# Output projection of a hybrid decoder layer: block products by a Strassen-Winograd scheme in place of eight block products, with prepared weight blocks kept in DRAM

## The chip, the core and the metric

The kernel runs on one core of a Trainium2 chip. The metric is the time of one execution in device microseconds; it was measured in three runs and the median counts. The engines are named as in the profile: PE is the matmul engine, PEld its weight loads, DVE the vector engine, ACT the scalar engine, POOL the GpSimd engine, and SP the queue that issues nearly all transfers between DRAM and SBUF, the on-chip memory. PSUM is the memory into which PE accumulates, in banks of 128 x 512 numbers.

## The reference

One layer is computed for x of 2048 tokens by 1024 columns, in float32. One projection feeds three token mixers, and their outputs go side by side through the output projection, which is added to the scaled input and normalised:

```python
    h = jnp.einsum('bsd,de->bse', x, w_in)
    a_u, a_v, a_g, b_val, b_glu, b_g, c_q, c_f, c_i, c_g = jnp.split(h, offsets, axis=-1)
    y_a = _sgu_mixer(a_u, a_v, sgu_ln_g, sgu_ln_b, sgu_w, sgu_b) * jax.nn.silu(a_g)
    y_b = _conv_module(b_val, b_glu, conv_w, conv_b, conv_ln_g, conv_ln_b) * jax.nn.silu(b_g)
    y_c = _hgrn2_mixer(c_q, c_f, c_i, lb, hgrn_norm_g) * jax.nn.silu(c_g)
    y = jnp.concatenate([y_a, y_b, y_c], axis=-1)
    y = jnp.einsum('bse,ed->bsd', y, w_out)
    return _layernorm(DEEPNORM_ALPHA * x + y, post_ln_g, post_ln_b)
```

Branch A (256 columns) is a gated unit that mixes 128 positions of a chunk by a triangular matrix. Branch B (256) is a causal convolution of width 31. Branch C (512, four heads) is a gated linear recurrence in chunks of 64 positions. W_out is 1024 x 1024.

## The kernel before

**Numbers in two parts.** A float32 operand of a product is split into a high part, rounded to the format that PE multiplies in one pass, and the low rest. `split` (L142 to L144) casts the high part on ACT and subtracts on DVE. `three` (L199 to L202) makes one product of three matmuls: high by high, high by low and low by high, each 128 x 128 by up to 512 columns. `load_split` (L146 to L154) brings every such operand through raw buffers of 128 x 512, six in turn (`RAWB`), by DMAs on SP (L152), and splits each piece. `load_small` gives a weight of 1024 columns four pairs of buffers in turn (tags whi and wlo). `load_x` brings a group of 512 tokens of x, transposed, into the pairs xhi and xlo, of which there are two.

**Stages.** The 2048 tokens are four groups of 512, and two groups make a half (`hf`). Each half goes through branch B, branch A, the values of branch C (`values`, L343 to L348: 16 products of 24 matmuls with 256 columns, copied out by ACT), and then C's eight units: four heads by two groups (`hgrn_unit`). A unit has projections f, q and g by `proj_f` (24 matmuls of 512 columns into one of three banks with the tag mm), elementwise work on DVE and ACT (among it L355, L362 and L377), score matmuls (L398) and small matmuls for states. Branch B's convolution runs on DVE as 31 multiply-adds of 128 x 512 for each of four accumulations per half (L284), put out one by one beside the later branches at the distance `DTAP` on the program's clock, and branch A's unit (`sgu_unit`) mixes at L629. `rstd_of` (L226 and L227) makes the reciprocal root of a variance on POOL. Every branch stores its output, transposed, to the DRAM tensor y_dr through SP (`y_store`, L231).

**Output projection.** In half 2 W_out is loaded and split: its left 512 columns (woh, wol) at the last head of C, its right 512 columns (xhiwo, xlowo) into the buffers of an x group after the last use. Then sixteen token tiles of 128 follow (from L738). For each, all 1024 columns of y come back as two DMAs of 256 KB, are split, and 2 x 24 matmuls go into two banks (po). L755 adds the scaled x, which L745 loaded, to a bank's result, L758 takes statistics, L760 joins them, POOL makes the reciprocal root, L762 and L765 normalise 1024 columns in two passes, and L766 stores them. The last tile's right half is done in two pieces of 256 columns, so that the end is short.

**What sets the order.** A clock counts the matmuls that the program has written (`tick`), and work is put off by `later` until the clock passes. A scheduler then orders the instructions of each engine by its own estimate, except those that are pinned to the written order. Each engine goes through its list in that order.

## Time and profile before

| what | value |
|---|---|
| median of three runs | 951.6 us (949.56 to 952.94) |
| the profiled execution: its span | 948.6 us |
| PE busy | 932.0 us, 98% of the span, 6165 matmuls |
| DVE busy | 668.3 us, 70% |
| ACT busy | 339.3 us, 36% |
| POOL busy | 83.0 us, 9% |
| memory read and written | 60.32 MB and 16.78 MB |

The profiled execution's own time is its span, 948.6 us; the runs of the table's first line were timed around the whole execution. A group row of the profile names the line, the engine, the operation, what it writes and reads, the shape and how often, and then the busy time, the mean of one in ns, the idle time of the engine just before and what ended it. A timeline row has the start and the duration in us first. A window row has the stretch, its length, the busy time of PE, PEld, DVE, ACT and POOL (with the count of instructions), PE's granted clock as a share of full speed, the DMA engines' busy share and GB/s. The stages of half 1 begin at about 0 (B), 75 (A), 148 (values) and 196 us (C), those of half 2 at 400, 453, 525 and 573 us, and the output projection at 753 us, at first between C's last units.

### The profile page before, as it was taken

The numbers are of one execution on the slowest core, as the hardware profiler recorded it, in microseconds if no ns is written. First come the engines' busy times: TensorE is split into PE (matmuls) and PEld (weight loads), VectorE is DVE, ScalarE is ACT, GpSimd is POOL, SyncE is SP. The second block draws the span as 40 slices with busy tenths as digits, with TensorE's granted clock in tenths as the row PEclk, the third lists the DMA queues.
The fourth block names the chain that finished last, engine by engine and source line by source line (L and its number), as shares of the span: only waits on it lengthen the run. The fifth ranks groups of instructions, "written<-read, shape, count | busy, mean of one in ns | idle before, by whom it ended". The sixth has DMA issues, their size and how long they took to land.

```text
span 948.6 us, 15705 instructions
## 1 busy us (share of the span) xinstructions
PE 932.0 (98%) x6165; PEld 772.7 (81%) x6165; DVE 668.3 (70%) x1561; ACT 339.3 (36%) x698; POOL 83.0 (9%) x130
## 2 busy tenths in 40 slices
PE   8999999999999999999999999999999999999996
PEld 5889889987777777788988998777777778888885
DVE  5998895146687669898899414668786965566554
ACT  6432333233354456552234223435455522110000
POOL 1001101000100000000210100010000012111211
PEclk9999999999999999999999999999999999999999
DMA  8401113111111104320111211201230734344221
GB/s 262 150 33 47 45 45 100 57 45 45 35 49 53 56 24 157 124 86 23 47 45 56 90 57 45 60 21 56 80 122 18 219 132 144 133 133 152 94 100 55
DMA packets 49993, 78.10 MB, mean 82 GB/s; under 512 B 4320, under 2 KB 20832, under 8 KB 49792
## 3 DMA queue, kind: packets, MB, share of 16 engines
q1 hardware_dynamic: 49872, 77.00, 24.8%
q8 instruction: 48, 0.79, 0.3%
q14 instruction: 25, 0.20, 0.1%
q0 software_dynamic: 48, 0.11, 0.1%
HBM read 60.32 MB, written 16.78 MB: 81 GB/s over the span
## 4 chain that ended last, share of the span: by engine, by line
PE 86%; DVE 8%; ACT 2%; issue 1%; DMA 1%; POOL 0%; SPq 0%; DVEq 0%; POOLq 0%; ACTq 0%
PE po L200 6%; PE po L201 6%; PE po L202 6%; PE pm_ci L200 3%; PE pm_ci L202 3%; PE pm_ci L201 3%; PE pm_q L200 3%; PE pm_q L201 3%; PE pm_q L202 3%; PE pm_f L200 2%; PE pm_f L202 2%; PE pm_f L201 2%; PE pm_cg L200 2%; PE pm_cg L201 2%; PE pm_cg L202 2%; PE pm_u L200 2%
## 5 line engine op out<-in xcount | busy, mean ns | idle before, releaser
L284 DVE SCALAR_TENSOR_TENSOR acc<-bh,vec,acc 128x512 f32<-128x512 f32 x240 | 172.8, 743 | 2.6
L144 DVE TENSOR_TENSOR wl<-rw,wh 128x512 fp32r<-128x512 f32 x84 | 56.7, 685 | 58.1 <-ACT wh L143 58.0
L143 ACT CAST wh<-rw 128x512 fp32r<-128x512 f32 x84 | 49.9, 618 | 42.5 <-PE pm_f L201 11.1
L755 DVE SCALAR_TENSOR_TENSOR rbuf<-rbuf,po 128x512 f32<-128x512 f32 (+1 forms) x33 | 22.1, 669 | 60.8 <-PE po L202 60.7
L200 PE MATMUL pm_ci<-wh_ci,xhix 128*128 128x256 f32 x192 | 54.8, 286 | 0.0
L202 PE MATMUL pm_ci<-wh_ci,xlox 128*128 128x256 f32 x192 | 54.3, 283 | 0.0
L201 PE MATMUL pm_ci<-wl_ci,xhix 128*128 128x256 f32 x192 | 54.3, 283 | 0.0
L200 PE MATMUL po<-xhiwo,wh_y 128*128 128x512 f32 (+1 forms) x136 | 52.2, 384 | 0.0
L143 ACT CAST wh_y<-rwy 128x512 fp32r<-128x512 f32 x32 | 18.6, 618 | 93.4 <-PE po L201 91.5
L201 PE MATMUL po<-xlowo,wh_y 128*128 128x512 f32 (+1 forms) x136 | 51.4, 378 | 0.0
L200 PE MATMUL po<-woh,wh_y 128*128 128x512 f32 x128 | 51.4, 401 | 0.0
L202 PE MATMUL po<-xhiwo,wl_y 128*128 128x512 f32 (+1 forms) x136 | 51.3, 377 | 0.0
L201 PE MATMUL po<-wol,wh_y 128*128 128x512 f32 x128 | 50.8, 397 | 0.0
L202 PE MATMUL po<-woh,wl_y 128*128 128x512 f32 x128 | 50.6, 395 | 0.0
L226 POOL TENSOR_SCALAR crs<-ss 128x4 f32<-128x4 f32 x16 | 3.6, 225 | 443.3 <-ACT jk L551 443.3
L200 PE MATMUL pm_f<-xhix,wh 128*128 128x512 f32 x96 | 41.0, 427 | 0.0
L200 PE MATMUL pm_q<-xhix,wh 128*128 128x512 f32 x96 | 40.9, 426 | 0.0
L201 PE MATMUL pm_q<-xlox,wh 128*128 128x512 f32 x96 | 39.3, 409 | 0.0
L200 PE MATMUL pm_cg<-xhix,wh 128*128 128x512 f32 x96 | 38.7, 403 | 0.0
L202 PE MATMUL pm_f<-xhix,wl 128*128 128x512 f32 x96 | 37.7, 393 | 0.0
L202 PE MATMUL pm_q<-xhix,wl 128*128 128x512 f32 x96 | 37.7, 393 | 0.0
L201 PE MATMUL pm_f<-xlox,wh 128*128 128x512 f32 x96 | 37.7, 393 | 0.0
(284 smaller groups left out, 2642.2 us busy)
## 6 DMA issues: line engine op xcount, KB each, us to landing
rw<-wf SPq DMA_DIRECT2D x84, 256.0 KB, 2.9
rwy<-y_dr SPq DMA_DIRECT2D x32, 256.0 KB, 3.7
rbuf<-x SPq DMA_DIRECT2D x16, 512.0 KB, 3.5
out<-rbuf SPq DMA_DIRECT2D x15, 512.0 KB, 2.6
rx<-xT SPq DMA_DIRECT2D x24, 256.0 KB, 3.5
rwci<-wt SPq DMA_DIRECT2D x16, 256.0 KB, 2.8
y_dr<-sg SPq DMA_DIRECT2D x16, 256.0 KB, 2.4
rwo<-wout SPq DMA_DIRECT2D x16, 256.0 KB, 2.9
```

Of the source, the lines that this page charges most:

```text
L143: nc.scalar.copy(hi, src)
L144: nc.vector.tensor_sub(lo, src, hi.bitcast(F32))
L200: nc.tensor.matmul(out, wh, xh, start=first, stop=False)
L201: nc.tensor.matmul(out, wh, xl, start=False, stop=False)
L202: nc.tensor.matmul(out, wl, xh, start=False, stop=last)
L226: nc.gpsimd.tensor_scalar(r, mv_var, scale, EPS, ALU.mult, ALU.add)
L284: nc.vector.scalar_tensor_tensor(a, h[:, k : k + G], vcol(cw + k), a, ALU.mult, ALU.add)
L755: nc.vector.scalar_tensor_tensor(r[:, ns], xn[:, ns], ALPHA, pt, ALU.mult, ALU.add)
```

## The change

**Seven products for eight.** A pair of token tiles is a 2 x 2 block matrix of y: a11 and a12 are the first tile's columns 0 to 511 and 512 to 1023, a21 and a22 the second's. W_out is a 2 x 2 block matrix too. The result is formed by the Winograd form of Strassen's scheme: four sums of y blocks (s1 to s4, on POOL), four of W_out's blocks, seven block products of 12 matmuls each (4 x `three`) and seven sums of products. Eight pairs take the place of sixteen tiles. The bank z accumulates four products, and ACT copies its state out in between (u1, u2, u4); the bank a holds one product and the bank dd two. DVE adds them into the tiles of x (xr).

**W_out's blocks.** `wo_prep` runs in half 1, in four steps behind the products 0, 4, 8 and 12 of `values`: it reads two rows of 512 KB of W_out, makes four sums on DVE, splits the seven blocks, and writes the high and low parts to the DRAM tensor wo_dr by 56 DMAs of 256 KB in all, 14.7 MB. `wo_load` brings a block back as two DMAs of 1 MB: blocks 0 to 2 into a new pool when C's pools are closed, 3 and 4 into the buffers of x's group 2, 5 and 6 into those of group 3, each when branch A has used that group for the last time.

**The order of half 2** becomes B, values, C, A; in half 1 it stays B, A, values, C. **Raw buffers** become three of 1024 columns, so most operands come and are split in pieces of 1024 instead of 512; the twelve first pieces of the program stay 512 wide. `DTAP` becomes 1.35 in half 2. The last tile's result is no longer cut into 256 columns.

```diff
-RAWB = 6
+RAWB = 3
...
-DTAP, DNORM = 1.5, 8.0
+DTAP, DNORM = (1.5, 1.35), 8.0
...
+    wo_dr = dr.tile([7, P, 2, 4 * 512], F32, name="wo_dr")
...
     def load_split(nm, hi, lo, srcs):
...
-            raw = wp.tile([P, 512], F32, tag="raw", bufs=RAWB, name=f"r{nm}_{k}")
+            raw = wp.tile([P, 1024], F32, tag="raw", bufs=RAWB, name=f"r{nm}_{k}")
+            n = src.shape[1] * (src.shape[2] if len(src.shape) == 3 else 1)
+            raw = raw[:, :n]
...
     def load_x(g):
-        return load_big(f"x{g}", [d["xT"][kt, :, g * G : (g + 1) * G] for kt in range(KT)])
+        return load_big(f"x{g}", [d["xT"][kt : kt + 2, :, g * G : (g + 1) * G]
+                                  .rearrange("k p t -> p k t") for kt in range(0, KT, 2)])
...
-    def values(hf, xs, vh):
+    def values(hf, xs, vh, between=lambda n: None):
...
+                    between(vp * 8 + gi * 4 + tt)
...
+    def wo_prep(pl, j):
+        raw = []
+        for e in range(2):
+            r = pl.tile([P, 1024], F32, tag="wr", bufs=2, name=f"wr{j}_{e}")
+            nc.sync.dma_start(r, d["wout"][:, j + 4 * e, :])
+            raw.append(r)
+        b11, b12 = raw[0][:, :512], raw[0][:, 512:]
+        b21, b22 = raw[1][:, :512], raw[1][:, 512:]
+        ta = pl.tile([P, 1024], F32, tag="wt", bufs=2, name=f"wta{j}")
+        tb = pl.tile([P, 1024], F32, tag="wt", bufs=2, name=f"wtb{j}")
+        t2, t3, t1, t4 = ta[:, :512], ta[:, 512:], tb[:, :512], tb[:, 512:]
+        nc.vector.tensor_sub(t1, b12, b11)
+        nc.vector.tensor_sub(t3, b22, b12)
+        nc.vector.tensor_sub(t2, b22, t1)
+        nc.vector.tensor_sub(t4, b21, t2)
+        for k, (src, blks) in enumerate(((b11, (0,)), (raw[1], (1, 5)), (ta, (2, 3)), (tb, (4, 6)))):
+            n = 512 * len(blks)
+            hi = pl.tile([P, 1024], F32R, tag="wh", bufs=2, name=f"wsh{j}_{k}")
+            lo = pl.tile([P, 1024], F32R, tag="wl", bufs=2, name=f"wsl{j}_{k}")
+            split(src, hi[:, :n], lo[:, :n])
+            for q, blk in enumerate(blks):
+                sl = slice(q * 512, (q + 1) * 512)
+                for hl, t in enumerate((hi, lo)):
+                    nc.sync.dma_start(wo_dr[blk, :, hl, j * 512 : (j + 1) * 512],
+                                      t[:, sl].bitcast(F32))
+    wo = [None] * 7
+    def wo_load(blk, t):
+        tv = t.bitcast(F32)
+        for k in range(2):
+            sl = slice(k * 1024, (k + 1) * 1024)
+            nc.sync.dma_start(tv[:, :, sl], wo_dr[blk, :, :, sl])
+        wo[blk] = t
...
+    def sgu(hf, xs, pl, after):
+        ws = [load_w(d["wt"][0, j], f"av{hf}_{j}") for j in range(2)]
+        vhat = sgu_values(hf, xs, pl, ws)
+        w = [load_wf(o, hf) for o in (A_U, A_G, A_U + 1, A_G + 1)]
+        for gi in range(GPH):
+            sgu_unit(hf * GPH + gi, gi, xs[gi], pl, vhat, w)
+            after(gi)
...
+            with ExitStack() as esa:
+                pl = pool(f"a{hf}", stack=esa, reuse_waits="tile")
+                sgu(hf, xs, pl, lambda gi: None)
+            with ExitStack() as esw:
+                pl = pool("wos", stack=esw, reuse_waits="tile")
+                values(hf, xs, vh, lambda n: wo_prep(pl, n // 4) if n % 4 == 0 else None)
...
+    def free_c(gi):
+        if gi == 0:
+            assert live[0] == 0
+            esc.close()
+            esv.close()
+            w1 = pool("w1", stack=es, reuse_waits="tile")
+            for blk in range(3):
+                wo_load(blk, w1.tile([P, 2, 4 * 512], F32R, name=f"wob{blk}"))
+            stiles.extend(w1.tile([P, 1024], F32, name=f"ysum{k}") for k in range(2))
+        for k, tag in enumerate(("xhi", "xlo")):
+            blk = 3 + 2 * gi + k
+            wo_load(blk, xp.tile([P, 2, 4 * 512], F32R, tag=tag, bufs=2, name=f"wob{blk}"))
+    stiles = []
+    with ExitStack() as esa:
+        pl = pool("a1", stack=esa, side="right", reuse_waits="tile")
+        sgu(NHALF - 1, xs, pl, free_c)
+    NP = S // (2 * P)
+    ot = pool("ot", stack=es, side="right", reuse_waits="tile")
+    gb = ot.tile([P, 2, DM], F32, name="gb")
     nc.sync.dma_start(gb, d["post"])
-    smp = pool("smp", stack=es)
-    for t in range(S // P):
-        yw = load_small(f"y{t}", [
-            y_dr[4 * j : 4 * j + 4, :, t * P : (t + 1) * P].rearrange("k p t -> p k t")
-            for j in range(2)])
...
-            pt = bank("mm", 3, f"po{t}_{n}_{c0}")[:, :w]
-            for kt in range(KT):
-                three(pt, yh[:, kt, :], yl[:, kt, :], wo[n][0][:, kt, c0 : c0 + w],
-                      wo[n][1][:, kt, c0 : c0 + w], kt == 0, kt == KT - 1)
-                tick(0.64 * w / 512)
...
+    def y_blocks(p):
+        raws = []
+        for k in range(2):
+            r = wp.tile([P, 1024], F32, tag="raw", bufs=RAWB, name=f"ry{p}_{k}")
+            t0 = (2 * p + k) * P
+            nc.sync.dma_start(r.rearrange("p (k t) -> p k t", t=P),
+                              y_dr[:, :, t0 : t0 + P].rearrange("k p t -> p k t"))
+            raws.append(r)
+        a11, a12 = raws[0][:, :512], raws[0][:, 512:]
+        a21, a22 = raws[1][:, :512], raws[1][:, 512:]
+        s2, s3 = stiles[0][:, :512], stiles[0][:, 512:]
+        s1, s4 = stiles[1][:, :512], stiles[1][:, 512:]
+        nc.gpsimd.tensor_tensor(s1, a21, a22, ALU.add)
+        nc.gpsimd.tensor_tensor(s2, s1, a11, ALU.subtract)
+        nc.gpsimd.tensor_tensor(s3, a11, a21, ALU.subtract)
+        nc.gpsimd.tensor_tensor(s4, a12, s2, ALU.subtract)
+        out = []
+        for k, src in enumerate((raws[0], stiles[0], stiles[1], a22)):
+            n = src.shape[1]
+            hi = wp.tile([P, 1024], F32R, tag="whi", bufs=4, name=f"wh_y{p}_{k}")
+            lo = wp.tile([P, 1024], F32R, tag="wlo", bufs=4, name=f"wl_y{p}_{k}")
+            split(src, hi[:, :n], lo[:, :n])
+            for q in range(n // 512):
+                sl = slice(q * 512, (q + 1) * 512)
+                out.append([t[:, sl].rearrange("p (k t) -> p k t", t=P) for t in (hi, lo)])
+        return dict(zip(("a11", "a12", "s2", "s3", "s1", "s4", "a22"), out))
+    def product(out, y, blk, first):
+        w = wo[blk].rearrange("p h (k n) -> p h k n", n=512)
+        for kt in range(4):
+            three(out, y[0][:, kt, :], y[1][:, kt, :], w[:, 0, kt, :], w[:, 1, kt, :],
+                  first and kt == 0, kt == 3, skip_group_check=not first)
+            tick(0.64)
+    def tmp(nm):
+        return ot.tile([P, 512], F32, tag="tmp", bufs=4, name=nm)
+    def normed(t, r, fine):
+        st = smp.tile([P, 2, 6], F32, tag="ost", bufs=2, name=f"ost{t}")
+        for n in range(2):
+            nc.vector.bn_stats(st[:, n, :], r[:, n * 512 : (n + 1) * 512])
         mv = smp.tile([P, 2], F32, tag="omv", bufs=2, name=f"omv{t}")
+        nc.vector.bn_aggr(mv, st)
         rs = rstd_of(smp, mv[:, 1:2], 1, "ors")
         nc.vector.scalar_tensor_tensor(r, r, mv[:, 0:1], gb[:, 0, :], ALU.subtract, ALU.mult)
+        for n in range(2 if fine else 1):
+            ns = slice(n * 512, (n + 1) * 512) if fine else slice(0, DM)
             nc.vector.scalar_tensor_tensor(r[:, ns], r[:, ns], rs, gb[:, 1, ns], ALU.mult, ALU.add)
             nc.sync.dma_start(d["out"][t * P : (t + 1) * P, ns], r[:, ns])
+    smp = pool("smp", stack=es, side="right")
+    n0, n1 = slice(0, 512), slice(512, 1024)
+    for p in range(NP):
+        y = y_blocks(p)
+        xr = []
+        for k in range(2):
+            t = 2 * p + k
+            r = ot.tile([P, DM], F32, tag="xr", bufs=4, name=f"xr{t}")
+            nc.sync.dma_start(r, d["x"][t * P : (t + 1) * P, :])
+            xr.append(r)
+        r1, r2 = xr
+        def plus(r, ns, t):
+            nc.vector.scalar_tensor_tensor(r[:, ns], r[:, ns], ALPHA, t, ALU.mult, ALU.add)
+        def join(r, ns, bk):
+            nc.vector.tensor_add(r[:, ns], r[:, ns], bk)
+        z = bank("mm", 3, f"poz{p}")
+        a = bank(("o", "st")[p % 2], 1, f"poa{p}")
+        dd = bank("sc", 2, f"pod{p}")
+        product(z, y["a11"], 0, True)
+        u1 = tmp(f"u1_{p}")
+        nc.scalar.copy(u1, z)
+        plus(r1, n0, u1)
+        product(a, y["a12"], 1, True)
+        join(r1, n0, a)
+        product(z, y["s2"], 2, False)
+        u2 = tmp(f"u2_{p}")
+        nc.scalar.copy(u2, z)
+        plus(r2, n0, u2)
+        product(dd, y["s3"], 3, True)
+        plus(r2, n1, dd)
+        product(z, y["s1"], 4, False)
+        u4 = tmp(f"u4_{p}")
+        nc.scalar.copy(u4, z)
+        nc.vector.tensor_add(r2[:, n1], r2[:, n1], u4)
+        product(dd, y["a22"], 6, False)
+        join(r2, n0, dd)
+        normed(2 * p + 1, r2, False)
+        product(z, y["s4"], 5, False)
+        plus(r1, n1, z)
+        normed(2 * p, r1, p == NP - 1)
```

Three places show how the engines' orders change. First ACT, at the end of half 1's values. `vh` takes the values (pm_ci), `wh` is a weight's high part, `f` and `X` are the first C unit's, and `wsh` are the high parts of W_out's blocks, from raw rows `wr` and sums `wta`, `wtb`. Before:

```order
L348 COPY vh<-pm_ci_1_1_2_1772 128x256
L143 CAST wh_0_1856<-rw_0_0_1858 128x512
L143 CAST wh_0_1856<-rw_0_1_1862 128x512
L348 COPY vh<-pm_ci_1_1_3_1800 128x256
L143 CAST wh_0_2188<-rw_0_0_2190 128x512
L143 CAST wh_0_2188<-rw_0_1_2194 128x512
L355 ACT_TABLE_LOAD
L355 ACTIVATE f_0_1895<-pm_f_0_1866 128x512
```

With the change:

```order
L354 COPY vh<-pm_ci_1_1_3_1892 128x256
L145 CAST wh_0_2269<-rw_0_0_2271 128x1024
L145 CAST wsh_3_1676<-wtb_1649 128x1024
L145 CAST wsh_0_1806<-wr_0_1796 128x512
L145 CAST wsh_1_1812<-wr_1_1798 128x1024
L145 CAST wsh_2_1820<-wta_1800 128x1024
L145 CAST wsh_3_1828<-wtb_1801 128x1024
L362 ACT_TABLE_LOAD
L362 ACTIVATE f_0_1976<-pm_f_0_1947 128x512
```

Five casts of W_out's blocks, those of the last step and one of the step before, now stand between the last value and `f` of the first C unit.

Second SP, where the output projection begins. Before, `rwo` are raw pieces of W_out, `rwy` of y, `gbb` the two vectors of the last normalisation, `rbuf` a tile of x, and y_dr takes the last outputs of C:

```order
L231 DMA y_dr<-sg_3_6585 128x512
L152 DMA rwo_6_7457<-wout 128x512
L152 DMA rwo_7_7461<-wout 128x512
L152 DMA rwy_0_7713<-y_dr 128x4x128
L152 DMA rwy_1_7717<-y_dr 128x4x128
L152 DMA rwy_0_7887<-y_dr 128x4x128
L152 DMA rwy_1_7891<-y_dr 128x4x128
L231 DMA y_dr<-sg_2_6877 128x512
```

With the change `wob` are W_out's blocks, in the order of their numbers 0 to 6, `ay` outputs of branch A, `xr` tiles of x and `ry` tiles of y:

```order
L237 DMA y_dr<-ay_2_7507 128x512
L713 DMA wob_7592<-wo_dr 128x2x1024 x2
L713 DMA wob_7595<-wo_dr 128x2x1024 x2
L237 DMA y_dr<-ay_2_7583 128x512
L713 DMA wob_7598<-wo_dr 128x2x1024 x2
L713 DMA wob_7603<-wo_dr 128x2x1024 x2
L713 DMA wob_7606<-wo_dr 128x2x1024 x2
L237 DMA y_dr<-ay_3_7675 128x512
L713 DMA wob_7747<-wo_dr 128x2x1024
L237 DMA y_dr<-ay_3_7744 128x512
L713 DMA wob_7747<-wo_dr 128x2x1024
L713 DMA wob_7750<-wo_dr 128x2x1024 x2
```

Behind these follow gb, both x tiles of pair 0 and the second y tile of pair 1 (ry_1_7914). The loads of W_out moved behind branch A's stores, and x, which stood behind the first tiles of y, stands behind all blocks.

Third DVE, in a steady stretch of the output projection. Before, one token tile:

```order
L755 SCALAR_TENSOR_TENSOR rbuf<-rbuf,po_0_0_8431 128x512
L758 BN_STATS ost_8430<-rbuf 128x6
L755 SCALAR_TENSOR_TENSOR rbuf<-rbuf,po_1_0_8458 128x512
L144 TENSOR_TENSOR wl_y_8716<-rwy_0_8717,wh_y_8715 128x512
L758 BN_STATS ost_8430<-rbuf 128x6
L144 TENSOR_TENSOR wl_y_8716<-rwy_1_8721,wh_y_8715 128x512
L760 BN_AGGR omv_8485<-ost_8430 128x2
L762 SCALAR_TENSOR_TENSOR rbuf<-rbuf,omv_8485,gbb 128x1024
L765 SCALAR_TENSOR_TENSOR rbuf<-rbuf,ors,gbb 128x1024
```

With the change, from the split of the next pair's s1 and s4 (`wl_y_2`) to the first sums of the next pair (`xr_8386`):

```order
L146 TENSOR_TENSOR wl_y_2_8379<-ysum_7602,wh_y_2_8378 128x1024
L838 SCALAR_TENSOR_TENSOR xr_8238<-xr_8238,omv_8330,gb 128x1024
L857 SCALAR_TENSOR_TENSOR xr_8236<-xr_8236,poz_8240 128x512
L841 SCALAR_TENSOR_TENSOR xr_8238<-xr_8238,ors,gb 128x1024
L834 BN_STATS ost_8351<-xr_8236 128x6
L146 TENSOR_TENSOR wl_y_3_8383<-ry_1_8364,wh_y_3_8382 128x512
L836 BN_AGGR omv_8354<-ost_8351 128x2
L857 SCALAR_TENSOR_TENSOR xr_8386<-xr_8386,u_4_8405 128x512
L838 SCALAR_TENSOR_TENSOR xr_8236<-xr_8236,omv_8354,gb 128x1024
L860 TENSOR_TENSOR xr_8386<-xr_8386,poa_8391 128x512
L841 SCALAR_TENSOR_TENSOR xr_8236<-xr_8236,ors,gb 128x1024
```

The normalising passes of two tiles now stand together, beside the splits and the first sums of the next pair.

More of the change, by code (lines that the diff above doesn't have):

```diff
@@ L152, in load_split @@
             nc.sync.dma_start(rv, src)
-            sl = slice(k * 512, (k + 1) * 512)
-            split(raw, hi[:, sl], lo[:, sl])
+            split(raw, hi[:, at : at + n], lo[:, at : at + n])
+            at += n
     def load_big(nm, srcs):
```

68 lines of the change are left out of this document (15 added, 53 removed).

## The prediction

> **What bounds the kernel now.** I read the page first, then the chain of waits, then stage windows and timelines. From the page:
>
> ```profile
> span 948.6 us, 15705 instructions
> PE 932.0 (98%) x6165; PEld 772.7 (81%) x6165; DVE 668.3 (70%) x1561; ACT 339.3 (36%) x698; POOL 83.0 (9%) x130
> PE   8999999999999999999999999999999999999996
> PEclk9999999999999999999999999999999999999999
> q1 hardware_dynamic: 49872, 77.00, 24.8%
> PE 86%; DVE 8%; ACT 2%; issue 1%; DMA 1%; POOL 0%; SPq 0%; DVEq 0%; POOLq 0%; ACTq 0%
> ```
>
> The reader is to see that TensorE (PE) is the bound in every slice but the first and the last, at full granted clock, and that 86% of the chain that ended last is PE. So whatever takes matmuls away shortens the run, as long as no other engine comes due in their place. DVE is next with 70%. The profiled execution spans 948.6 us; the median of the runs is 951.6, so about 3.0 us lie around the span. I work on the span and add 3.0. No change means within 0.3% of 951.6, that is 948.7 to 954.5.
>
> **1. The matmuls that go.** Starts of the first matmul of W_out half 0 (woh), of half 1 (xhiwo), and of the next token tile:
>
> ```profile
> 840.79 0.40 PE L200 MATMUL po<-woh,wh_y 128*128 128x512 f32 x1
> 846.39 0.39 PE L200 MATMUL po<-xhiwo,wh_y 128*128 128x512 f32 x1
> 851.86 0.40 PE L200 MATMUL po<-woh,wh_y 128*128 128x512 f32 x1
> ```
>
> A half is 24 matmuls: 5.60 us for woh (0.2333 each), 5.47 for xhiwo (0.2279). A tile is 11.07, so 16 tiles take 177.1 us for 768 matmuls. After, 8 pairs of 84 make 672. At the mean of 0.2306 that is 155.0, **-22.1 us**; at the two rates -20.3 to -24.0, since I cannot tell which rate the new places in SBUF get. A pair takes 19.1 to 19.6, I use 19.4.
>
> **2. The start.** The raw buffers become 3 of 1024 columns instead of 6 of 512, and the twelve first pieces stay 512 wide, so only three are in flight.
>
> ```profile
> 0.79 0.39 SPq L152 DMA_DIRECT2D rwfirst<-wf  x1
> 3.44 0.62 ACT L143 CAST whi_first<-rwfirst 128x512 fp32r<-128x512 f32 x1 [1.37 <-DMA rwfirst<-wf]
> 4.09 0.69 DVE L144 TENSOR_TENSOR wlo_first<-rwfirst,whi_first 128x512 fp32r<-128x512 f32 x1 [2.78 <-ACT whi_first L143]
> 20.49 0.39 PE L200 MATMUL pm_bg<-xhi_first,wh 128*128 128x512 f32 x1
> ```
>
> A buffer's round is issue to end of subtraction, 0.79 to 4.78: 4.0 us. Four rounds of three put the last split at about 17 to 19 us; PE's first two projections end at 20.5 today. So the twelve pieces are nearly hidden; the next weight comes as one 512 KB piece and is late by about **+1** (0 to +3).
>
> **3. W_out's sums during half 1's C values (wo_prep).** This adds work beside PE.
>
> ```profile
> 148.00:196.00 48.00, 48.00 (x399) 47.84 (x399) 11.82 (x22) 12.68 (x28) 2.54 (x6) 1.00 0.18 61
> 841.59 0.69 DVE L144 TENSOR_TENSOR wl_y<-rwy,wh_y 128x512 fp32r<-128x512 f32 x1
> 842.20 0.69 DVE L758 BATCH_NORM_STATS2 ost<-rbuf 128x6 f32<-128x512 f32 x1
> 840.76 1.14 ACT L143 CAST wh_y<-rwy 128x512 fp32r<-128x512 f32 x2 [9.93 <-PE po L201]
> 200.75 0.60 ACT L355 ACTIVATE f<-pm_f 128x512 f32<-128x512 f32 x1 [2.75 <-PE pm_f L202]
> 201.37 1.28 ACT L362 ACT_TABLE_LOAD   x1
> 206.19 0.69 ACT L362 ACTIVATE X<-pm_q 128x512 f32<-128x512 f32 x1 [3.54 <-PE pm_q L202]
> 211.52 0.76 PE L398 MATMUL sc<-X,K 128*32 128x80 f32 x32
> ```
>
> The first row is the values stage (columns PE, PEld, DVE, ACT, POOL, clock, DMA share, GB/s). A DVE subtraction of 512 occupies 0.61 from start to start, one of 1024 about 1.14 by doubling all but the fixed part. Each of four steps is 4 subtractions (2.4), one split of 512 (0.6) and three of 1024 (3.4): 6.4, in all 26 us of DVE; ACT casts 4 x (0.57 + 3 x 1.1) = 15.5 us. DVE is idle 36 of these 48 us and ACT 35, so the engines hide it. DMA does not: 4.2 MB of W_out are read, 14.7 MB written (7 x 128 x 2 x 2048 x 4 bytes), 2.1 MB are weights. The queue row gives 77.00 MB in 24.8% of 948.6 us, 327 GB/s while packets move: 21 MB are 64 us in a stage of 48. In ACT's order the last five casts stand ahead of f of the first C unit, and the last one waits until the writes two buffers back have landed: 19.4 MB, 59 us from 150, 2 to land, so 211, and 212 with its cast. Then follow 1.28 + 0.60 (table, f), 1.28 + 0.69 (table, X) and about 2 us of DVE (three operations of the size of L377 in point 6): scores at 218. PE starts its 16 score groups at 211.5 today; seven more matmuls stand ahead of them now, 1.6 us: 213. That is +5; at 367 GB/s (point 5) nothing. I take **+4** (0 to +9).
>
> **4. Branch A of half 2 behind C.** A and the values leave and enter with all their instructions; PE's work is the same. Less PE work now stands between branch B and C, in which the convolution must end.
>
> ```profile
> L284 DVE SCALAR_TENSOR_TENSOR acc<-bh,vec,acc 128x512 f32<-128x512 f32 x240 | 172.8, 743 | 2.6
> 431.63 0.69 DVE L259 TENSOR_TENSOR bh<-pm_val,bsig 128x512 f32<-128x512 f32 x1 [4.60 <-PE pm_val L202]
> 433.44 10.02 DVE L284 SCALAR_TENSOR_TENSOR acc<-bh,vec,acc 128x512 f32<-128x512 f32 x15
> L200 PE MATMUL pm_av<-wh_av,xhix x47: 278/283/283, 453.1 to 469.7; 128*128 128x256 f32 x47
> ```
>
> After 431.6 three of the four accumulations remain: 93 taps at 10.02 / 15 = 0.67 are 62 us, with eight splits (9) and a few multiplies 73: DVE is free at about 506. Then come branch B's statistics, about 5 us. PE leaves B at 453 (the first matmul of A today); with 48 for the values and two projections of 5.4 C's first X is due at 512. This is just covered: **0**, +4 if DVE is late, -1 since W_out's loads no longer disturb C's last head.
>
> **5. Reloading seven blocks and the first pair.** SP's order (with the change) has blocks 0 and 1 behind half 2's first y store of branch A, 2 to 4 behind its second, 5 and 6 behind its last; gb, x and pair 1's second y load stand behind all of them.
>
> ```profile
> 7.00:9.00 2.00, 1.14 (x4) 0.44 (x3) 1.00 (x2) 1.57 (x3) 0.00 (x0) 1.00 1.02 367
> 487.22 1.02 PE mix L629 x16
> ...
> 524.10 1.02 PE mix L629 x16
> rbuf<-x SPq DMA_DIRECT2D x16, 512.0 KB, 3.5
> ```
>
> The first and the last of four mixes stand 36.9 us apart, 12.3 each. Counting from A's first u projection, they lie at 12, 24, 36 and 48.5, PE is through at 49.3, and stores follow some 3 us behind. Blocks 0 to 4 (10.5 MB) are asked for from 18 on; at 340 GB/s, between 327 and 367, they run until 50. Blocks 5 and 6 can't start before x's buffers are free (48.3), nor the last before the store at 52. With gb, x and y 6.8 MB remain: 20 us, x of pair 0 at 68 to 70, pair 1's y at 71. PE has work until 71 from blocks that are there (the scheduler put pieces of pair 1 between). DVE needs x for its first sum, and four operations later (3 us) the bank of a22 is free: PE waits 0.6. The sums of pair 1 want three POOL additions, a cast and a split after 71: 77 against 74.4. With some catching up, **+4** (0 to +11).
> The Trainium skill (DMA: Bandwidth & Descriptors, Specifications) gives about 358 GB/s as the limit of a core's HBM traffic; the queue row's 327 lies under it, the two-microsecond row's 367 over it. By 358 this term would be about +3 as an estimate.
>
> **6. The steady pairs.** PE no longer waits for one sum at the end; seven products share two banks, and DVE has twice the split work per matmul (7 widths of 512 for 84, before 4 for 96). Rows that price DVE and POOL:
>
> ```profile
> 843.63 1.28 DVE L762 SCALAR_TENSOR_TENSOR rbuf<-rbuf,omv,gbb 128x1024 f32<-128x1024 f32 x1
> 843.68 1.28 POOL L226 TENSOR_SCALAR ors<-omv 128x1 f32<-128x1 f32 x1 [9.15 <-DVE omv L760]
> 845.63 1.29 DVE L765 SCALAR_TENSOR_TENSOR rbuf<-rbuf,ors,gbb 128x1024 f32<-128x1024 f32 x1 [0.72 <-POOL ors L227]
> 846.83 0.68 DVE L755 SCALAR_TENSOR_TENSOR rbuf<-rbuf,po 128x512 f32<-128x512 f32 x1
> 847.55 0.69 DVE L758 BATCH_NORM_STATS2 ost<-rbuf 128x6 f32<-128x512 f32 x1
> 249.98 0.58 DVE L377 TENSOR_TENSOR X<-X,f 128x256 f32<-128x256 f32 x1
> L226 POOL TENSOR_SCALAR crs<-ss 128x4 f32<-128x4 f32 x16 | 3.6, 225 | 443.3 <-ACT jk L551 443.3
> L584 POOL TENSOR_SCALAR_AFFINE_SELECT wm<-wm 128x512 f32<-128x512 f32 x1 | 1.0, 1025 | 20.1 <-DMA wm<-sguw 20.1
> ```
>
> From start to start: L765 1.20, L755 (PSUM) 0.72; statistics last as long as a split, 0.6; a tap is 0.67. ACT has 5.6 us a pair and is no bound. DVE's order has one tight loop: the split of the next pair's (s1,s4) waits until s4's product is over, since the buffer is the same, and from there the queue runs without a gap to the sum that frees a22's bank: cast 1.2, split 1.14, four normalising passes 4.8, sums and copies 0.72 + 0.65 + 0.7 + 0.65 + 0.72, statistics 0.8, splits 0.6 + 1.14: 13.1 us. PE gets to a22 five products after s4, at 13.8. So DVE fits with 0.7 us to spare, while POOL makes three of its four additions inside this stretch. No row shows such an addition; the nearest, L584, is 1.0 us. Whether it holds DVE up is open: L226 next to L762 takes 1.28, on a tile four times as wide but away from such DVE work 0.225, and ends as DVE ends, so the two exclude each other in one direction, while L377 started next to a POOL operation and ran at its usual 0.58. Bounds: nothing, or 3 x 1.0 - 0.7 = 2.3 us for each of 7 pairs, 16. In the stretch 2.7 us of DVE operations read only one SBUF operand and can lie beside POOL, so I take 1 us a pair: **+7** (0 to +16).
> The Trainium skill (SBUF — State Buffer, Who interferes with whom) says that a DVE instruction with two SBUF inputs and a GpSimd one that reads SBUF exclude each other, the first to start holding the port pair for its whole length. By that rule the L226 row agrees, additions hold DVE in turn, and the sum goes to the upper half of this range, as an estimate +12.
>
> **7. The end.** After the last matmul:
>
> ```profile
> 940.88 0.43 DVE rbuf L755
> ```
>
> The last sum is 512 wide, not 256 (0.72 for 0.43), so are its statistics (+0.2), and in DVE's order the other tile's last pass (1.2) stands between them: **+1.7** (1 to 2.5).
>
> Sum: -22.1 + 1 + 4 + 0 + 4 + 7 + 1.7 = -4.4. Three of these losses can't all be at their middle: the prep and pair 0 lose together by slow DMA, the loop by the port; where DMA is fast both of the first fall to 1 or 2. I put the likeliest at -6.6: 942.0 of span, **945 us**.
>
> **Rivals.** (a) *POOL's additions don't hold DVE.* Then term 6 is 0 and the time is 945 - 7 = 938; 935 if DMA also runs near 367. For: the L377 row. Against: the L226 row. (b) *The port becomes the bound, slower than before.* Every addition costs DVE its full length and DVE falls behind by 2.3 us or more a pair; with the fourth addition and L226's two beside the normalising passes, up to 3 us: 7 x 3 = 21 instead of 7, giving 959. It decides from 2.1 us of stall a pair on: 14.7 + the other 10.7 exceed 22.1 by 3.3, over 0.3%. (c) *DMA bound at both ends.* At 262 GB/s, the mean of the page's first slice (GB/s row below), the 17.3 MB from 18 on take 66 us, x lands at 86 instead of 70, +16 for +4, and the prep +9: 945 + 12 + 5 = 962.
>
> ```profile
> GB/s 262 150 33 47 45 45 100 57 45 45 35 49 53 56 24 157 124 86 23 47 45 56 90 57 45 60 21 56 80 122 18 219 132 144 133 133 152 94 100 55
> ```
>
> For: that slice was 84% busy. Against: it waits for buffers too, and packets of 2 KB and more moved faster elsewhere. (d) *The change doesn't shorten PE's queue*: excluded by the count, 672 for 768.
>
> **Chances.** Forecast 0.47 (940 to 950), (a) 0.24, (b) 0.16, (c) 0.13. The forecast's own range lies mostly under 948.7 (0.34 of 0.47), the rest within 0.3%; with (a) faster is 0.58; of (b) and (c) milder forms give 0.03 to no change, the rest is slower. So faster 0.58, same 0.16, slower 0.26. The range 935 to 958 holds (a), the forecast and the milder half of (b) and (c).
>
> **What would show it.** Right: 84 matmuls a pair at 0.228 to 0.233; the first scores of half 1 late by a few us behind ACT's casts; PE idle near the first pair for DMA or DVE; a22 waiting for DVE once a pair; POOL additions of 1 us or longer. Wrong: DVE idle in the steady pairs (then (a)); pairs of 21 us and more (then (b)); x of pair 0 landing over 30 us after branch A's last matmul (then (c)); PE waiting in branch B or C of half 2, which I hold covered.

## The result and the profile after

The changed kernel takes 966.8 us (964.45 to 970.7, four runs) against 951.56 us of the kernel before (949.56 to 952.94, four runs): a ratio of 1.0168, 95% interval 1.0141 to 1.0195. It is slower by 1.7%, where 945 us had been forecast. The profiled execution spans 964.8 us, 16.2 more than before. From its page:

```profile
span 964.8 us, 15346 instructions
PE 919.1 (95%) x6045; PEld 758.4 (79%) x6045; DVE 726.4 (75%) x1532; ACT 365.0 (38%) x658; POOL 134.4 (14%) x162
PE   7999999996999999999999999999999998899995
PEclk9999999997999999999999999999999999899998
q1 hardware_dynamic: 52368, 106.36, 32.6%
PE 59%; DVE 21%; DMA 9%; issue 4%; ACT 3%; POOL 3%; SPq 1%; DVEq 0%; POOLq 0%; ACTq 0%
```

PE's work did shrink, but PE's share of the chain that ended last fell from 86% to 59%: DVE and DMA stand in it now. The slices show where: the first, the tenth (217 to 241 us, where the granted clock falls too), the 34th and 35th (796 to 844 us) and the last. Windows make this sharper:

```profile
154.60:202.00 47.40, 47.40 (x398) 47.40 (x397) 26.22 (x36) 17.88 (x30) 0.89 (x2) 1.00 0.83 288
202.00:230.00 28.00, 20.75 (x109) 16.41 (x112) 17.88 (x28) 13.19 (x16) 1.19 (x3) 0.87 0.91 335
...
785.40:812.00 26.60, 24.75 (x105) 19.77 (x104) 9.06 (x13) 4.69 (x7) 3.00 (x3) 0.96 0.94 327
812.00:830.00 18.00, 12.04 (x47) 8.99 (x46) 14.32 (x17) 5.69 (x7) 12.80 (x10) 0.88 0.28 89
...
890.00:910.00 20.00, 20.00 (x90) 16.55 (x89) 19.24 (x24) 5.55 (x7) 10.84 (x8) 1.00 0.56 173
```

From 154 to 230 us the DMA engines are busy 83 to 91% of the time, and PE loses 7 us at the end of it. The output projection begins at 785.4: PE loses 2 and 6 us in its first 45 us. Between 850 and 890 us it loses 2.7 more. From 890 us on PE is busy all the time, although DVE is busy 19.24 us of 20. What PE waited for longest:

```profile
PE pod L206 <- DVE xr L857: 9.2, 4, 4.6
PE pm_f L206 <- ACT f L362: 5.8, 1, 5.8
```

To divide the 16.2 us, the same point of the program is sought in both traces: the first matmul of branch A, the first scores of C, the last matmul of half 2's branch B, the first and the last of the output projection. Before:

```profile
L200 PE MATMUL pm_av<-wh_av,xhi_first x32: 283/283/387, 75.6 to 86.8; 128*128 128x256 f32 x32
L398 PE MATMUL sc<-X,K x1024: 206/232/257, 211.5 to 761.2; 128*32 128x80 f32 x86, 128*32 128x48 f32 x85
L202 PE MATMUL pm_bg<-xhix,wl x32: 389/389/397, 393.0 to 452.9; 128*128 128x512 f32 x32
L200 PE MATMUL po<-xhiwo,wh_y x136: 280/389/504, 760.1 to 940.3; 128*128 128x512 f32 x120, 128*128 128x256 f32 x16
```

And after:

```profile
L206 PE MATMUL pm_av<-wh_av,xhi_first x32: 277/283/283, 82.7 to 93.8; 128*128 128x256 f32 x32
L405 PE MATMUL sc<-X,K x1024: 206/232/342, 229.2 to 709.8; 128*32 128x80 f32 x86, 128*32 128x48 f32 x85
L208 PE MATMUL pm_bg<-xhix,wl x32: 388/389/395, 413.1 to 473.1; 128*128 128x512 f32 x32
L206 PE MATMUL poz<-wob,wh_y x128: 388/389/499, 785.4 to 953.3; 128*128 128x512 f32 x128
```

The start is late by 7.1 us. By the first scores it is 17.7, so the preparation costs 10.6. By the end of half 2's branch B it is 20.2: another 2.5 in C of half 1. Before, the output projection's 177.1 us of matmuls would have filled the time from 763.7 to 940.8; now they begin at 785.4, late by 21.7: another 1.5 for the new order of half 2. The last matmul ends at 954.1: the projection takes 168.7 us. In it 12 matmuls in a row take 2.72 us (818.55 to 821.27 us), 0.2267 each, so 672 are 152.3: PE's saving is 24.8, and 16.4 are lost again. Behind the last matmul 10.7 us remain instead of 7.8: 2.9. The sum: 7.1 + 10.6 + 2.5 + 1.5 - 24.8 + 16.4 + 2.9 = 16.2.

How the preparation holds PE, in the timeline of ACT and then of PE:

```profile
216.18 0.62 ACT L145 CAST wsh<-wr 128x512 fp32r<-128x512 f32 x1 [8.61 <-DMA wr<-wout]
...
221.36 1.04 ACT L145 CAST wsh<-wtb 128x1024 fp32r<-128x1024 f32 x1 [0.90 <-DMA wo_dr<-wsh]
222.43 1.28 ACT L362 ACT_TABLE_LOAD   x1
223.72 0.60 ACT L362 ACTIVATE f<-pm_f 128x512 f32<-128x512 f32 x1
```

```profile
224.37 0.80 PE L206 MATMUL pm_f<-xhix,wh 128*128 128x512 f32 x1 [5.81 <-ACT f L362]
224.97 0.63 PE L207 MATMUL pm_f<-xlox,wh 128*128 128x512 f32 x1
225.39 0.63 PE L208 MATMUL pm_f<-xhix,wl 128*128 128x512 f32 x1
```

`f` of the first C unit stands behind the last casts of W_out's blocks on ACT, and these wait for DMA (8.61 us at one place). PE has all three mm banks full and waits 5.81 us for `f` to free one. Behind the wait the matmuls start 0.42 us apart instead of 0.227.

And the first pairs, from the timelines of DVE, POOL and PE:

```profile
806.30 0.69 DVE L857 SCALAR_TENSOR_TENSOR xr<-xr,u 128x512 f32<-128x512 f32 x1 [13.02 <-DMA xr<-x]
...
820.33 2.20 DVE L838 SCALAR_TENSOR_TENSOR xr<-xr,omv,gb 128x1024 f32<-128x1024 f32 x1
```

```profile
809.00 1.27 POOL L806 TENSOR_TENSOR ysum<-ry 128x512 f32<-128x512 f32 x1 [51.54 <-DMA ry<-y_dr]
...
821.40 2.27 POOL L807 TENSOR_TENSOR ysum<-ysum,ry 128x512 f32<-128x512 f32 x1
```

```profile
829.43 0.79 PE L206 MATMUL pod<-wob,wh_y 128*128 128x512 f32 x1 [4.60 <-DVE xr L857]
830.02 0.63 PE L207 MATMUL pod<-wob,wh_y 128*128 128x512 f32 x1
```

DVE stands idle for 13.02 us until x of pair 0 is there, the second y tile of pair 1 lands at 809.0, and from then on two pairs' sums, splits and normalising passes lie on DVE at once, beside POOL's additions. A 1024-wide pass takes 2.20 us where it met an addition, and an addition 2.27 where it met a pass, against 1.28 and 1.27. PE waits 4.60 us for a bank that DVE has not read, and again runs slowly behind it. Part of this wait is not DVE's work but POOL's order:

```profile
825.44 0.19 POOL L232 TENSOR_SCALAR ors<-omv 128x1 f32<-128x1 f32 x1
826.29 1.28 DVE L841 SCALAR_TENSOR_TENSOR xr<-xr,ors,gb 128x1024 f32<-128x1024 f32 x1 [2.08 <-POOL ors L233]
```

The variance for this pass, of a tile of pair 0, is there at 819.9, but POOL begins its reciprocal root only at 825.44, behind the additions of pair 2. DVE stands idle for 2.08 us, and the sum that frees PE's bank stands behind this pass in DVE's order. The chain of waits that leads to the matmul at 829.43 runs through the late loads of y, POOL's additions, this root and DVE's passes.

### The profile page after: what moved, and what is told of

Same layout as the page of the kernel before. It is cut to its first block, busy times and chain, and to the rows that moved or that the text cites. A ratio compares the mean times of both kernels' runs of the same rounds, so it can differ in the third digit from the quotient of the medians.

```text
span 964.8 us, 15346 instructions
## 1 busy us (share of the span) xinstructions
PE 919.1 (95%) x6045; PEld 758.4 (79%) x6045; DVE 726.4 (75%) x1532; ACT 365.0 (38%) x658; POOL 134.4 (14%) x162
## 4 chain that ended last, share of the span: by engine, by line
PE 59%; DVE 21%; DMA 9%; issue 4%; ACT 3%; POOL 3%; SPq 1%; DVEq 0%; POOLq 0%; ACTq 0%
DVE acc L290 4%; PE pm_q L206 3%; PE pm_q L207 2%; PE pm_q L208 2%; PE pm_f L206 2%; DMA wr<-wout 2%; PE pm_f L207 2%; PE pm_f L208 2%; DMA ry<-y_dr 2%; PE pm_cg L206 2%; DVE wl L146 2%; PE poz L208 2%; PE poz L207 2%; PE poz L206 2%; PE pm_ci L208 2%
## 5 line engine op out<-in xcount | busy, mean ns | idle before, releaser
L146 DVE TENSOR_TENSOR wl<-rw,wh 128x1024 fp32r<-128x1024 f32 x42 | 51.3, 1223 | 20.1 <-ACT wh L145 20.0
L145 ACT CAST wh<-rw 128x1024 fp32r<-128x1024 f32 x42 | 44.1, 1049 | 33.6 <-PE pm_f L207 12.6
L206 PE MATMUL poz<-wob,wh_y 128*128 128x512 f32 x128 | 50.0, 392 | 0.7 <-ACT wh_y L145 0.7
L208 PE MATMUL poz<-wob,wl_y 128*128 128x512 f32 x128 | 49.6, 390 | 0.6 <-DVE wl_y L146 0.6
L207 PE MATMUL poz<-wob,wh_y 128*128 128x512 f32 x128 | 49.8, 389 | 0.0
L558 ACT ACTIVATE jk<-po 128x128 f32<-128x128 f32 x64 | 17.7, 276 | 57.4 <-PE po L553 56.5
L207 PE MATMUL pm_f<-xlox,wh 128*128 128x512 f32 x96 | 38.7, 404 | 0.0
L208 PE MATMUL pm_f<-xhix,wl 128*128 128x512 f32 x96 | 38.7, 403 | 0.0
L208 PE MATMUL pm_cg<-xhix,wl 128*128 128x512 f32 x96 | 37.5, 390 | 0.0
L207 PE MATMUL pm_cg<-xlox,wh 128*128 128x512 f32 x96 | 37.5, 390 | 0.0
L207 PEld LDWEIGHTS pm_ci<-wl_ci,xhix 128*128 128x128 f32 x192 | 36.9, 192 | 0.0
L206 PEld LDWEIGHTS pm_ci<-wh_ci,xhix 128*128 128x128 f32 x192 | 36.9, 192 | 0.0
```

The costliest lines, as they stand in the source:

```text
L145: nc.scalar.copy(hi, src)
L146: nc.vector.tensor_sub(lo, src, hi.bitcast(F32))
L206: nc.tensor.matmul(out, wh, xh, start=first, stop=False, **kw)
L207: nc.tensor.matmul(out, wh, xl, start=False, stop=False, **kw)
L208: nc.tensor.matmul(out, wl, xh, start=False, stop=last, **kw)
L558: nc.scalar.activation(jk, po[:, c * P : (c + 1) * P], AF.Square, accum_out=ss[:, c : c + 1])
```

## The experiments

Theory A: the matmuls go as counted; the time is lost at the start by the raw buffers, in half 1 by the preparation's bytes, and in the first pairs by late x and y with POOL's additions on top. Its rivals were that DVE or POOL bounds the steady pairs, or that latency and order, not bytes, set the two DMA stages. All ratios are against the kernel before; with the changed kernel's 1.0168, one hundredth of ratio is 9.5 us.

**Raw buffers undone.** Pieces of 512 columns, two to a raw buffer, so six in flight:

```diff
-        for k, src in enumerate(srcs):
-            raw = wp.tile([P, 1024], F32, tag="raw", bufs=RAWB, name=f"r{nm}_{k}")
...
+                if not half:
+                    t = wp.tile([P, 1024], F32, tag="raw", bufs=RAWB, name=f"r{nm}_{k}")
+                    half.extend((t[:, :512], t[:, 512:]))
+                raw = half.pop(0)
```

> The changed kernel, with operands cut into pieces of 512 columns again; two pieces share one of the three raw buffers of 1024, so six are in flight. Theory A (the start is late because only three pieces are in flight, and the next x group waits for its own larger pieces): the first matmul of branch A comes at about 76 us instead of 82.7, and the time falls by 6 to 8 us, to about 960. Rival B (the first pieces are late for the speed of the DMA engines alone, or the delay is taken up later by a wait that is there anyway): first matmul of branch A later than 80, or the time falls by less than 3 us.

Measured: 1.0114 (1.0085 to 1.0142), about 5 us less than the changed kernel. The first matmul of branch A is at 76.1, as before the change:

```profile
L219 PE MATMUL pm_av<-wh_av,xhi_first x32: 283/283/388, 76.1 to 87.3; 128*128 128x256 f32 x32
```

The start is the raw buffers'. Of the 6.6 us won there 4.5 are left at the first scores (224.7): the preparation's first read came only 3.8 us earlier (156.5), and its last cast's end 4.7 (217.7).

**The raw buffers alone, in the kernel before.** `RAWB = 3`, tiles and pieces of 1024:

> The kernel before with the raw buffers alone changed: three of 1024 columns, pieces of 1024 except the twelve first. Theory A (this edit by itself makes the start late): first matmul of branch A at 80 to 85 us instead of 75.6, time higher by 4 to 8 us, about 957. Rival B (the late start needs the other edits): time within 2 us of the kernel before.

Measured: 1.0125 (1.01 to 1.0149), some 12 us, more than expected. The first matmul of A is at 80.2 (4.6 late), B of half 2 ends 7.2 late, the output projection ends 10.7 late. So the start is only part of it: here the larger pieces cost 2.6 us more between branch A of half 1 and branch B of half 2, and 3.5 behind that. The preparation took back some of what undoing them won in the changed kernel; why the rest was not won there stays open. Over all runs with three buffers the first matmul of A lies between 79.8 and 84.9 us, with six always between 75.6 and 76.2.

**Half the preparation's bytes.** Only the high parts are written, and the reload reads them twice:

```diff
-                for hl, t in enumerate((hi, lo)):
-                    nc.sync.dma_start(wo_dr[blk, :, hl, j * 512 : (j + 1) * 512],
-                                      t[:, sl].bitcast(F32))
+                nc.sync.dma_start(wo_dr[blk, :, 0, j * 512 : (j + 1) * 512],
+                                  hi[:, sl].bitcast(F32))
```

> The changed kernel, but only the high parts of the block sums are written to DRAM (7.3 MB for 14.7) and the reload reads them for both parts; all casts and subtractions of the preparation stay. The low parts of the weights are so left out of the result. Theory A (the preparation in half 1 is bound by its DMA bytes, and the last five casts on ACT hold the first forget gate f of branch C): the first scores come at about 221 instead of 229.2 and the time falls by 7 to 10 us, to about 958. Rival B (the chain of reads, casts and two buffers is bound by latency, whatever the bytes): scores later than 226 and the time falls by less than 4 us.

Measured: 1.0068 (1.0048 to 1.0088), 9.5 us less. In this run the first matmul of A is at 84.9, 9.3 later than in the kernel before, and the scores are late by 9.5:

```profile
L405 PE MATMUL sc<-X,K x1024: 206/232/257, 221.0 to 701.5; 128*32 128x80 f32 x86, 128*32 128x48 f32 x85
```

So with half the writes the preparation costs nothing, although all its casts still run ahead of `f`: they are over at 208.8 us instead of 222.4. It was bound by DMA, not by the chain of casts and buffers. Bytes and the count of writes fell together here; what speaks for the bytes is that, from the first read to the last cast, the DMA engines moved 286 GB/s over 46.2 us here and 317 GB/s over 62.1 us in the changed kernel: at a similar rate the length fell with the bytes.

**The y sums.** First without them:

```diff
-        nc.gpsimd.tensor_tensor(s1, a21, a22, ALU.add)
...
-        for k, src in enumerate((raws[0], stiles[0], stiles[1], a22)):
+        for k, src in enumerate((raws[0], raws[1], raws[0], a22)):
```

> The changed kernel without the four block sums on POOL; the splits read the blocks of y instead, so the result lacks the sums, while DVE, ACT and PE have the same instructions. Theory A (additions of 1.3 to 2.3 us stand between the second pair's y and its products and hold DVE's two-operand instructions): PE's losses from 812 to 890 us, about 9 us with the lower clock behind them, mostly go, and the time falls by 5 to 9 us, to about 960. Rival B (the first two pairs wait for DMA only, and PE is the bound from 890 us on, so the additions are covered): the time falls by less than 3 us.

Measured: 1.0037 (1.0024 to 1.005), 12.5 us less, more than theory A gave it. x comes no earlier (DVE waits 13.1 us for it), but the projection takes 156.6 us instead of 168.7, because DVE and PE catch up at once:

```profile
830.00:850.00 20.00, 20.00 (x90) 16.57 (x89) 18.79 (x26) 5.55 (x7) 5.65 (x6) 1.00 0.53 177
```

Then with the additions made, but read by nothing:

> As the run without the additions (the splits read the blocks of y, so the sums are missing from the result), but POOL makes its four additions per pair all the same, into tiles that nothing reads. Theory A (what costs is mainly the additions' place in the chain from y's load to the products: their latency): the time stays near the run without additions, 954 to 957. Rival B (what costs is mainly that they hold DVE's instructions): DVE's steady pairs are as long as in the changed kernel, and most of the 12.5 us return: 960 to 966.

Measured: 1.0253 (1.0225 to 1.0281), slower than the changed kernel by 8 us. It is not their place in the chain of y alone that costs:

```profile
PE pod L206 <- DVE xr L857: 19.7, 6, 8.9
L841 DVE SCALAR_TENSOR_TENSOR xr<-xr,ors,gb 128x1024 f32<-128x1024 f32 x15 | 24.3, 1617 | 8.1 <-POOL ors L233 7.9
```

The pass takes 1617 ns on average, and DVE waits 7.9 us for the reciprocal roots (2.8 in the changed kernel), which queue behind the free-running additions on POOL. Last, the additions on DVE (`nc.vector` for `nc.gpsimd`):

> The changed kernel with the four block sums of y on DVE instead of POOL, everything else the same. Theory A (POOL's additions cost by their length, 1.3 us alone and up to 2.3 beside DVE, and by holding DVE, more than DVE's own 4 x 0.6 = 2.4 us per pair): DVE then works about 18.2 us per pair of 19.1, PE stays the bound in the steady pairs, and the time falls by 7 to 12 us against the changed kernel, to about 957. Rival B (DVE has no room for 2.4 us more and becomes the bound): pairs of 20 us and more, time not lower than 964.

Measured: 1.0135 (1.0116 to 1.0155), about 3 us less: neither theory's number. Even these do not come from the sums: the projection of the profiled run takes 169.3 us, no less than in the changed kernel, and the first matmul of A is at 79.8 instead of 82.7. DVE still waits 12.91 us for x, and then has the sums to make besides two pairs' work. Where the sums are made matters little while x is late.

**SP's order.** Blocks 5 and 6 and gb behind x of pair 0:

```diff
-        sgu(NHALF - 1, xs, pl, free_c)
+        sgu(NHALF - 1, xs, pl, lambda gi: None if gi else free_c(gi))
...
-    nc.sync.dma_start(gb, d["post"])
...
+        if p == 0:
+            free_c(1)
+            nc.sync.dma_start(gb, d["post"])
```

> The changed kernel with blocks 5 and 6 and the post-normalisation vectors asked for behind the x tiles of pair 0 in the program, which puts x ahead of block 6 and of the vectors on SP's queue. Theory A (PE waits in the first pairs for the sum that needs x, because x stands behind the blocks): x lands at about 797 instead of 806, PE waits for the third accumulation of the first pairs by 4 us less, and the time falls by 3 to 5 us, to about 963. Rival B (the bytes bound it: what x gains, block 6 and the second pair's y lose): the time stays within 2 us.

Measured: 1.012 (1.0105 to 1.0135), 4.6 us less in the runs, but the projection of the profiled run is shorter by only 3.3. The wait moved:

```profile
PE poz L206 <- ACT wh_y L145: 8.6, 1, 8.6
```

Now the second pair's sums are late instead of the first pair's x: POOL makes them from 808.6 to 817.0, the first two in 2.0 and 2.2 us beside DVE's passes.

**Half the reload's bytes**, the preparation untouched; DVE zeroes the low halves:

> The changed kernel, but the reload brings only the high halves of the seven blocks (7.3 MB for 14.7) and DVE sets the low halves to zero, 2048 columns per block; the low parts of the weights are so left out of the result. The preparation in half 1 is untouched. Theory A (the output projection's 168 us come from the reload's bytes, which make x and y of the first pairs late, and from the catching up behind it): x lands before PE needs it, the output projection takes 156 to 159 us, the time falls by 8 to 12 us, to about 956, while the first scores stay at 227 to 230. Rival B (the additions' latency and their hold on DVE bind the first pairs whatever lands when): less than 4 us.

Measured: 1.0079 (1.0056 to 1.0102), 8.5 us less, with the scores at 231.9 and the output projection shorter by 10:

```profile
L206 PE MATMUL poz<-wob,wh_y x128: 389/389/501, 785.0 to 942.7; 128*128 128x512 f32 x128
```

The two cures are not additive: fewer bytes alone give 10 of the projection's lost 16.4 us, no additions alone give 12.

**Unsplit sums in DRAM.** A true cure for both DMA stages: 4.2 MB written and 7.3 MB read back, and the split made at the reload:

```diff
+        for k, t in enumerate((ta, tb)):
+            nc.sync.dma_start(wo_dr[k, :, j, :], t)
...
+        load_split(f"wob{blk}", t[:, 0, :], t[:, 1, :], [src[:, :2], src[:, 2:]])
```

> The changed kernel, but the preparation in half 1 writes only the four sums, unsplit (4.2 MB for 14.7), and the seven blocks are split when they are loaded in half 2 (7.3 MB for 14.7), W_out's own blocks straight from W_out. Theory A (the preparation is bound by bytes and the reload too, while DVE and ACT have room beside branch A of half 2): first scores at about 220, x of pair 0 lands earlier, time lower by 9 to 14 us, about 955. Rival B (28 more splits beside branch A delay the first pairs on DVE and ACT by what the preparation gains): time lower by less than 5 us.

Measured: 1.004 (1.0028 to 1.0052), 12 us less. The scores come with no loss beyond the start's (84.5 for 75.6, 220.3 for 211.5), and the projection takes 158. But PE stands still before its first product:

```profile
PE poz L206 <- ACT wh_y L145: 9.6, 1, 9.6
```

y of pair 0 now stands behind the blocks' pieces, which share its raw buffers.

**The four cures together** (pieces of 512, unsplit sums, y sums on DVE, x ahead of block 6):

> Four repairs together: operands in pieces of 512 with six in flight, only unsplit sums in DRAM, the y sums on DVE, x ahead of block 6 on SP's queue. Theory A (the changed kernel's loss is the sum of the start, the preparation, the additions on POOL and the first pairs, and seven products for eight are worth about 24 us of PE): 5 + 10 + 10 + 2 us less than the changed kernel, about 939, faster than the kernel before by 1 to 1.5%. Rival B (the losses hide one another, or DVE becomes the bound of the output projection): not below 946.

Measured: 0.9821 (0.98 to 0.9843), 934.7 us: faster than the kernel before by 1.8% and than the changed kernel by 3.4%. The first matmul of A is at 75.7, the scores at 211.6, and the projection runs from 765.5 for 157 us. Its windows, and below those of the same kernel with the y sums on POOL:

```profile
785.00:805.00 20.00, 18.47 (x80) 14.67 (x79) 19.80 (x29) 6.17 (x8) 3.91 (x4) 1.00 0.48 168
805.00:825.00 20.00, 20.00 (x90) 16.54 (x90) 19.89 (x28) 6.41 (x8) 3.27 (x4) 1.00 0.53 169
825.00:845.00 20.00, 20.00 (x90) 16.58 (x89) 19.38 (x28) 5.70 (x8) 2.73 (x4) 1.00 0.57 174
```

```profile
785.00:805.00 20.00, 19.63 (x87) 15.90 (x85) 17.75 (x18) 6.16 (x8) 15.43 (x12) 1.00 0.55 186
805.00:825.00 20.00, 16.15 (x64) 13.26 (x65) 17.69 (x20) 4.72 (x7) 11.10 (x9) 0.91 0.31 102
825.00:845.00 20.00, 20.00 (x90) 16.54 (x89) 19.23 (x24) 5.55 (x7) 11.50 (x9) 1.00 0.55 174
```

> The kernel with the four repairs, but with the y sums back on POOL. Theory A (additions on POOL cost little while DVE is not behind; in the changed kernel DVE was behind because x and y of the first pairs came late): within 4 us of the kernel with four repairs, 934 to 939. Rival B (POOL's additions hold DVE in every pair and PE waits for it): 942 to 948.

Measured with POOL: 0.9925 (0.99 to 0.995), 10 us slower than with DVE. So the additions cost even when x is early, but in the first two pairs alone: counted by 84 matmuls, these take 25.0 and 25.2 us instead of 21.1 and 21.2, and from 825 us on PE is busy 20.00 of 20 in both. Rival B had the size right and the place wrong.

**The end.** The last product cut into two pieces of 256 columns, on top of the four cures:

> The kernel with the four repairs, and the very last product cut into two pieces of 256 columns, whose sums and statistics follow piece by piece. Theory A (the end after the last matmul, 10.7 us against 7.7 in the kernel before, holds a sum and statistics of 512 columns and one more pass): 1 to 2 us less than the kernel with four repairs, about 933. Rival B (the chain of rstd on POOL and the passes sets the end): no difference above 0.5 us.

Measured: 0.9844 (0.9817 to 0.9871), no gain: 10.3 us remain behind the last matmul, as without the cut. This is rival B's case. The last sums still stand behind the other tile's two passes in DVE's order, and the root on POOL and the last passes follow.

Half 2 with branch A ahead of C was not tried: blocks 0 to 2 lie where C's buffers were, and would have no room.

## Why the prediction was wrong, step by step

A span of 942.0 us was forecast and 964.8 measured, 22.8 more. Step 2 missed by 6.1, step 3 by 6.6, steps 5 and 6 together by 5.4, step 7 by 1.2; the 2.5 us in C of half 1 and the 1.5 for the new order stood at nothing; the shading took off 2.2; and the matmuls gave 2.7 more than forecast. In size the start and the preparation missed most. In mechanism two steps failed: step 2 left out a load that goes through the same buffers, and step 6 had the cost of the additions in the wrong pairs.

**1. Matmuls:** right in kind, a little better: -24.8 for -22.1. The last four pairs take 19.1 us and less, 0.2267 a matmul for all seven blocks, under both old rates.

**2. The start: wrong, +7.1 for +1.** The prediction counted the rounds of the twelve first pieces, found them "nearly hidden" and charged only the next weight. The twelve pieces end at about 21.3 instead of 17 to 19, and the next x group, 2 MB in four pieces, goes through the same three buffers, which the prediction put at nothing: its first projection ends 8 us later (from the tile view of both kernels, glu's last first-term matmul with that group starts at 30.7 before and at 38.7 after). The undone buffers showed the whole term.

**3. The preparation: right mechanism, mis-sized, +10.6 for +4.** The chain of ACT, the casts ahead of `f` and the byte bound were as told, except that the longest wait in it, 8.61 us, was for the read of the last step's rows, which SP issued at 210.49 behind earlier writes, and not for the writes two buffers back (0.9 us each). The length was as told too: from the first read at 160.3 to the last cast's end at 222.4 it is 62 us, where 150 to 212 had been worked out. But it began at 160.3, right behind branch A's last store, while PE's own due time moved by the 7 us of the start alone: 3 us more. Then the forecast took 4 of its own 5, and left out that PE runs at half rate behind a wait.

**4. The new order of half 2: +1.5 for 0,** inside its bounds. The 2.5 us in C of half 1 are in no step of the prediction. The convolution was out of the way in time: its last multiply-add ends at 525.8 us, which less the 20.2 by which branch B is late is 505.6, for 506 forecast.

**5 and 6. Reload and pairs: +16.4 for 11.** x landed 73 us after branch A's first projection, for 68 to 70 forecast, and the second y tile of pair 1 at 76, for 71. Without the additions the projection still lost 4.3 us (156.6 less 152.3), for +4: step 5 was right. Step 6 is the step that failed. The additions cost 12.1 us (168.7 less 156.6) for +7, and in other pairs than it said. It gave DVE 0.7 us of room in a steady pair, took 1 us of holding, and spread the loss over seven pairs. Counted by 84 matmuls, the first seven pairs take 19.3, 31.6, 21.1, 20.3, 19.1, 19.1 and 19.1 us, and without the additions 19.3, 22.9 and five times 19.0. So the second to the fourth pair lose 8.6, 2.1 and 1.3 us by the additions, and the later ones 0.1 and less.

This is not because the holding is small there. In each steady pair one pass of 1.28 us takes 2.23, one sum of 0.68 takes 1.66, and one split of 0.67 takes 1.17. The rows show the split of s1 and s4, the sum that frees a22's bank and a22's first matmul, then the split and the sum in the run without the additions:

```profile
896.24 1.17 DVE L146 TENSOR_TENSOR wl_y<-ysum,wh_y 128x1024 fp32r<-128x1024 f32 x1
909.40 0.68 DVE L857 SCALAR_TENSOR_TENSOR xr<-xr,pod 128x512 f32<-128x512 f32 x1
910.33 0.40 PE L206 MATMUL pod<-wob,wh_y 128*128 128x512 f32 x1
```

```profile
904.47 1.17 DVE L146 TENSOR_TENSOR wl_y<-ry,wh_y 128x1024 fp32r<-128x1024 f32 x1
916.04 0.69 DVE L853 SCALAR_TENSOR_TENSOR xr<-xr,pod 128x512 f32<-128x512 f32 x1 [0.81 <-PE pod L208]
```

With the additions this stretch of DVE's queue takes 13.8 us, and a22's matmul comes 0.25 us behind its end, 14.1 behind its start. Without them the stretch is 11.4 us, the wait for PE taken off. So the additions take 2.4 us a pair, over twice what was forecast, and there were 2.6 us of room instead of 0.7. The 13.1 us of the forecast held a cast of 1.2 that ACT makes ahead of time. Holding and room were both too small in the forecast, and what they leave for PE to wait in a steady pair is nothing instead of 1 us.

The additions cost where the loads are late. Alone, the late loads cost 4.3 us; the additions, with half the reload's bytes, cost at most 6.2 (158.5 less 152.3); together it was 16.4. Steps 5 and 6 were priced apart, but here they reinforce each other: the late loads make a backlog, and the additions stretch the time to work it off, by holding DVE and by standing ahead of the roots on POOL. How the 12.1 us divide between holding and roots is not shown; the one wait for a root in the first pairs is 2.08 us.

**7. The end: +2.9 for +1.7.** The terms were as told, but the last sum also had to wait 0.7 us for the other tile's first pass, which runs from 953.60 to 954.88.

**The shading.** The sum of the steps was -4.4, and the forecast was moved to -6.6 because the losses could not "all be at their middle". All of them but the reload (4.3 for 4) were above it. Rival (c) had the right places, but its rate was not met: the window of the first pairs moves 327 GB/s, not 262. Rival (b)'s steady stall did not happen in this kernel: PE waited for a22's bank in the first four pairs only, though DVE was held by as much a pair as (b) said.

## What to carry to other kernels

A change that takes 24.8 us from the bounding engine can lose 41 us where that engine is fed: price the fill of every stage (who holds the buffers, what stands ahead on the queue, what comes due first), not only the steady state. Keep what is staged in DRAM in its smallest form and split it where engines have room; that alone was worth 12 us here. When two late things meet on one engine, price them together.
